# A hybrid attention layer: the compression's input tile stored with the blocks as its innermost axis

## The chip, the cores and the metric

The kernel runs on one core of a Trainium2 chip. The metric is device time in microseconds (us), the median of several executions. One more execution, taken with the hardware profiler, gives the rows below.

## The reference

One decoder layer over 512 tokens of width 1024. One projection of x feeds two token mixers: sparse attention (NSA), and gated DeltaNet. Their outputs are gated, summed and projected, then comes a gated MLP. The change is in the first branch of the sparse attention, the compression: of the 512 tokens, 31 blocks of 32 tokens are taken at a step of 16, so that neighbours overlap by half. Each block of 32 x 64 numbers, plus a learned position term, goes through a small two-layer network, once for keys (i = 0) and once for values (i = 1), in each of two groups of heads:

```
n_cmp = (S - CMP_LEN) // CMP_STRIDE + 1            # 31 blocks of 32 tokens, step 16
cmp_idx = np.arange(n_cmp)[:, None] * CMP_STRIDE + np.arange(CMP_LEN)[None, :]
def compress(t, i):
    blk = t[:, :, cmp_idx] + cmp_pos[i]
    blk = blk.reshape(B, G, n_cmp, CMP_LEN * DH)
    return jax.nn.gelu(blk @ cmp_w1[i]) @ cmp_w2[i]
k_cmp, v_cmp = compress(kc, 0), compress(vc, 1)
```

## The kernel before

The engines are named as in the profile: PE is TensorE (PEld its weight load), DVE is VectorE, ACT is ScalarE, POOL is GpSimd, SP is SyncE, which issues the DMAs.

The input projection is made in units of 128 output columns (gemm_t): a weight tile (raw) comes by DMA, is split into a high and a low part (wh on ACT or DVE at L215/L217, wl on DVE or POOL at L219), and 24 matmuls of 512 columns (lines 229, 231 and 232) build one product in a PSUM tile gps. The steps of the two mixers are listed in the table ORDER with priorities, and a scheduler lays them out in one fixed sequence on each engine. Units of the projection whose results are wanted later fill PE between the steps of the mixers. An engine works through its sequence in order, and waits where an operand or a buffer isn't ready.

The step "c" is the compression (compressed, in the code below). Two units of the projection (16 for the keys, 17 for the values) leave 128 rows by 512 tokens each in PSUM. Eight copies on ACT (lines 666 and 667, four for each unit) bring them into the tile kv: a head group's 64 rows as they are into partitions 0 to 63, and the same rows moved by one token into partitions 64 to 127. So one column of kv holds two neighbouring tokens, and a block of 32 tokens is 16 such columns. The fifth slice of kv holds the position terms and zeros. Line 674 then makes 16 matmuls, one for each j, that add up in one PSUM tile (ph in the code, aps in the profile): the weights are w1[j], and the moving operand is 5 slices of kv with 31 columns each, 155 in all, taken 16 elements (64 bytes) apart. Operands are float32, and each matmul stands in the trace as two records of MATMUL and two of LDWEIGHTS, so 32 of each. The two w1 tiles sit in the pool's raw buffers.

What hangs on ph is a chain: the position terms (hb, L678), bias (cu, L681), GELU (L684 to L688), the copies gv (L691), the second layer (L695 and L701, on PE), and its copies kcb and vcb.

Around it in the sequence stands the first head of the DeltaNet mixer: gdn_mid multiplies keys by keys and by queries (L466, two halves of two matmuls with 256 columns each), whose results DVE takes as m and at (L468, L469). They share a pool of two PSUM buffers (dps) with the transposes of the decay (L386), which ACT reads at L459 (dt). gdn_tri then inverts a triangular matrix: lo and f (L478, L480), gx (L486), a matmul of gx (L488), its copy lx (L489), and 15 dependent steps on DVE (L495 and L496), which end in z (L498) and its transposes on PE (L386).

Of the kernel before, what the change touches and what calls it, by code (L numbers as in the profile page):

```python
# [10 lines left out]
F32 = mybir.dt.float32  # L11
F32R = mybir.dt.float32r
AF = mybir.ActivationFunctionType
# [4 lines left out]
S = 512  # L18
# [112 lines left out]
def body(ctx: ExitStack, tc: tile.TileContext, d, out):  # L131
    nc = tc.nc
    V, A, G, PE = nc.vector, nc.scalar, nc.gpsimd, nc.tensor

    def E(name, h, d="V"):

        return {"V": V, "G": G, "A": A}[ENGINE.get(f"{name}{h}", d)]

    def bc(ap, shape):
        return ap.to_broadcast(shape)  # L140
# [64 lines left out]
    def split_w(src, shape, eng, first=A):  # L205

        raw = wp.tile(shape, F32, name="raw", bufs=BUFS["raw"])
        nc.sync.dma_start(out=raw, in_=src)
        half = shape[1] // 2
        hi, lo = [], []  # L210
        for i in range(2):
            r = raw[:, i * half:(i + 1) * half]
            wh = wp.tile([128, half] + list(shape[2:]), F32R, name="wh", bufs=BUFS["wh"])
            if first is A:
                A.activation(wh, r, AF.Copy)  # L215
            else:
                first.tensor_copy(wh, r)  # L217
            wl = wp.tile([128, half] + list(shape[2:]), F32R, name="wl", bufs=BUFS["wl"])
            eng.tensor_tensor(wl, r, wh.bitcast(F32), op=OP.subtract)  # L219
            hi += [wh[:, k] for k in range(half)]  # L220
            lo += [wl[:, k] for k in range(half)]
        return hi, lo

    def product(ps, w, m, n):

        (wh, wl), (mh_, ml_) = w, m
        first = None
        for k in range(n):
            i = PE.matmul(ps, wh[k], mh_(k), start=(k == 0), stop=False)  # L229
            first = first or i  # L230
            PE.matmul(ps, wh[k], ml_(k), start=False, stop=False)  # L231
            PE.matmul(ps, wl[k], mh_(k), start=False, stop=(k == n - 1))  # L232
        return first
# [3 lines left out]
    def gemm_t(u, eng=None, after=None):  # L237
        w = split_w(d["wT"][u], [128, KD, 128], E("ws", u, "G"), E("wh", u, "A"))
        ps = gps()
        first = product(ps, w, (lambda k: xh[:, k, :], lambda k: xl[:, k, :]), KD)  # L240
        if after is not None:
            tc.add_manual_dep(first.ins, after.ins.name, mybir.DependencyInfo(
                mybir.DependencyClass.NoSync, mybir.DependencyReason.SCHED_ONLY), reason="its rows have no room before")
        return ps
# [407 lines left out]
    def compressed():  # L652
        cst_ = ExitStack()
        ct = pool(cst_, name="ct", bufs=1, side="left")
        kv = ct.tile([128, 5, S], F32, name="kv")
        w2 = nsa.tile([128, 128], F32, name="w2")
        nc.sync.dma_start(out=w2, in_=d["w2"])
        pos = nsa.tile([128, 2, 16], F32, name="pos")
        nc.sync.dma_start(out=pos, in_=d["pos"])
        V.memset(kv[:, 4, :], 0.0)  # L660
        V.tensor_copy(kv[:, 4, :64].rearrange("p (i j two) -> p i j two", i=2, two=2)[:, :, :, 0], pos)
        for i in range(2):
            ps = gemm_t(16 + i)
            for g in range(2):
                own = slice(g * 64, g * 64 + 64)
                A.activation(kv[0:64, 2 * i + g, :], ps[own], AF.Copy)
                A.activation(kv[64:128, 2 * i + g, 0:S - 1], ps[own, 1:S], AF.Copy)
        w1 = []
        for i in range(2):
            w1.append(wp.tile([128, 8, 128], F32, name="raw", bufs=BUFS["raw"]))  # L670
            nc.sync.dma_start(out=w1[i], in_=d["w1"][:, 8 * i:8 * i + 8].rearrange("p a b c -> p a (b c)"))
        ph = aps()
        for j in range(16):
            PE.matmul(ph[:, :155].rearrange("p (a n) -> p a n", a=5), w1[j // 8][:, j % 8],
                      kv[:, :, 2 * j:2 * j + 481:16], start=(j == 0), stop=(j == 15))
        cst_.close()
        hb = nsa.tile([128, 2], F32, name="hb")
        V.tensor_copy(hb[0:64, 0:1], ph[0:64, 124:125])  # L678
        V.tensor_copy(hb[64:128, 0:1], ph[64:128, 126:127])
        u = nsa.tile([128, 62], F32, name="cu")  # L680
        A.activation(u[0:64], ph[0:64, 0:62], AF.Identity, bias=hb[0:64, 0:1])  # L681
        A.activation(u[64:128], ph[64:128, 62:124], AF.Identity, bias=hb[64:128, 0:1])
        t = nsa.tile([128, 62], F32, name="ct")
        V.tensor_tensor(t, u, u, op=OP.mult)  # L684
        V.tensor_scalar(t, t, 0.044715, 1.0, op0=OP.mult, op1=OP.add)
        V.tensor_tensor(t, t, u, op=OP.mult)
        A.activation(t, t, AF.Tanh, scale=GELU_C)
        V.scalar_tensor_tensor(u, t, 1.0, u, op0=OP.add, op1=OP.mult)  # L688
        gv = nsa.tile([128, 2, 4, 32], F32, name="gv")
        V.memset(gv, 0.0)  # L690
        V.tensor_copy(gv[64:128, :, :, 0:31],  # L691
                      bc(u[64:128].rearrange("p (g n) -> p g n", g=2)[:, :, None, :], (64, 2, 4, 31)))
        V.memset(kcb, 0.0)
        pk = aps()
        PE.matmul(pk[:, :62], w2[0:64], u[0:64], start=True, stop=True)  # L695
        for g in range(2):
            A.activation(kcb[0:64, g, 0:31], pk[0:64, 31 * g:31 * g + 31], AF.Copy, scale=0.5)
            A.activation(kcb[64:128, g, 32:63], pk[64:128, 31 * g:31 * g + 31], AF.Copy, scale=0.5)
        pv = aps()
        for g in range(2):  # L700
            PE.matmul(pv[:, 64 * g:64 * g + 64], gv[64:128, g].rearrange("p a b -> p (a b)"), w2[64:128, 0:64],  # L701
                      start=True, stop=True)
        for g in range(2):
            A.activation(vcb[:, g, 0, :], pv[:, 64 * g:64 * g + 64], AF.Copy, scale=0.5)
            V.scalar_tensor_tensor(vcb[:, g, 1, :], pv[:, 64 * g:64 * g + 64], 0.5,
                                   vcb[:, g, 0, :].bitcast(F32), op0=OP.mult, op1=OP.subtract)
# [140 lines left out]
    for step in ORDER:  # L847
        f = {"c": compressed, "k": keys, "q": queries, "p": cmp_attn, "a": lambda h: attn(h, (0, 1, 2)), "b": lambda h: attn(h, (3, 4, 5)),
             "i": gdn_k, "j": gdn_q, "v": gdn_v, "m": gdn_mid, "n": gdn_tri, "y": gdn_gate,
             "o": gdn_out, "g": lambda i: merge(i, mgp)}[step[0]]  # L850
        with tc.high_priority(offset=-(at + SHIFT.get(step, 0))):
            p0 = tc.tile_snap_priority()
            f(*[int(i) for i in step[1:]])
            at += tc.tile_snap_priority() - p0
        if step == "c":
            yo = pool(early, name="yo", bufs=1, side="left")
            mgp = pool(early, name="mg", bufs=1, side="left")
# [28 lines left out]
    for m in range(8):  # L886
# [5 lines left out]
        for b in range(2):  # L892
            ps = pm.tile([128, S], F32, name=f"pm{b}")
# [61 lines left out]
    for t in range(TT):  # L955
# [6 lines left out]
        for i in range(2):  # L962
            if i == 1 and t:
                x1_both(t - 1)
            ps = pw.tile([128, S], F32, name=f"pw{i}")
# [39 lines left out]
    for p in range(NF):  # L1005
        g = []
        for b in range(2):
            if p < NE:
                ps = first[p, b][2]
            else:  # L1010
                wu = split_w(d["up"][p, :, b], [128, KD, 128], V)
                ps = pu.tile([128, S], F32, name=f"pu{b}")
# [4 lines left out]
            for i in (1, 0):  # L1017
                n = 2 - i
# [72 lines left out]
```

## Time and profile before

| | |
|---|---|
| median of 3 runs | 876.38 us (875.93, 876.38, 881.3) |
| the profiled execution | 879.48 us |
| its span, first to last instruction | 877.7 us |
| granted clock of TensorE, mean over the span | 0.988 of full speed |

The profiled execution spends 1.8 us outside its span. Its rows are times from the start of the span. A matmul's row gives its start and a length that reaches past the start of the next one, since matmuls are pipelined: what one of them costs PE is the distance from one start to the next, called pitch below.

### The profile page before, as it was taken

The page shows a single profiled execution, that of the slowest core. Times are in us where ns is not written, and L with a number is a line of the kernel's source. Part 1 is how long each engine was busy: PE and PEld are TensorE (multiplying, and loading weights), DVE is VectorE, ACT ScalarE, POOL GpSimd, SP SyncE. Part 2 cuts the span into 40 slices and gives each one's busy share as a digit, 9 for nine tenths or more (in the row PEclk, how much of TensorE's full clock was granted, in tenths as well). Part 3 has the DMA queues.
Part 4 walks back from the last instruction along what each step waited for, and adds up shares of the span by engine and source line. Part 5 has one row for each costly group of instructions (what it writes and reads, how often), then busy time and mean ns, then how long its engine had stood idle before and what let it go on. Part 6 is the DMA issues. An engine that isn't in the chain of part 4 may idle for free.

```text
span 877.7 us, 11725 instructions
## 1 busy us (share of the span) xinstructions
PE 847.1 (97%) x4292; PEld 698.2 (80%) x4292; DVE 562.6 (64%) x1159; ACT 384.8 (44%) x855; POOL 159.9 (18%) x141
## 2 busy tenths in 40 slices
PE   9899799999999999999999999999999999999996
PEld 8677678777777678888888898888888888888885
DVE  4755759995766987485457636777766677423337
ACT  5463268567446767443234104444444444322220
POOL 1232342324424320112100001111111111000001
PEclk9999799999999999999999999999999999999999
DMA  7323110101111001254356001333333323333322
GB/s 244 119 72 96 48 50 25 49 25 49 48 50 48 25 26 49 73 159 137 135 192 240 24 1 49 96 96 97 96 97 98 97 98 98 106 100 99 96 73 96
DMA packets 22954, 76.33 MB, mean 87 GB/s; under 512 B 3184, under 2 KB 3568, under 8 KB 22640
## 3 DMA queue, kind: packets, MB, share of 16 engines
q1 hardware_dynamic: 22896, 75.57, 26.9%
q8 instruction: 34, 0.56, 0.2%
q14 instruction: 24, 0.20, 0.1%
HBM read 73.47 MB, written 2.10 MB: 86 GB/s over the span
## 4 chain that ended last, share of the span: by engine, by line
PE 86%; DVE 9%; ACT 2%; issue 1%; DMA 1%; POOL 0%; SPq 0%; DVEq 0%; ACTq 0%; POOLq 0%
PE pu L229 9%; PE pu L231 9%; PE pu L232 9%; PE gps L229 7%; PE gps L232 7%; PE gps L231 7%; PE pdn L1036 5%; PE pdn L1034 5%; PE pdn L1035 5%; PE pout L805 2%; DVE tmp L495 2%; PE pw L969 2%; PE pw L970 2%; PE pm L232 2%; PE pm L231 2%; PE pw L968 2%
## 5 line engine op out<-in xcount | busy, mean ns | idle before, releaser
L215 ACT ACTIVATE wh<-raw 128x512 fp32r<-128x512 f32 (+1 forms) x198 | 122.6, 622 | 224.4 <-PE pu L231 99.3
L219 DVE TENSOR_TENSOR wl<-raw,wh 128x512 fp32r<-128x512 f32 (+1 forms) x172 | 134.5, 784 | 133.4 <-ACT wh L215 130.5
L229 PE MATMUL pu<-mh,wh 128*128 128x512 f32 (+1 forms) x384 | 142.7, 372 | 0.0
L231 PE MATMUL pu<-ml,wh 128*128 128x512 f32 (+1 forms) x384 | 142.6, 371 | 0.0
L232 PE MATMUL pu<-mh,wl 128*128 128x512 f32 (+1 forms) x384 | 142.6, 371 | 0.0
L229 PE MATMUL gps<-xh,wh 128*128 128x512 f32 x320 | 131.3, 411 | 0.8 <-DVE acc L372 0.5
L232 PE MATMUL gps<-xh,wl 128*128 128x512 f32 x320 | 130.4, 407 | 0.0
L231 PE MATMUL gps<-xl,wh 128*128 128x512 f32 x320 | 129.0, 403 | 0.0
L219 POOL TENSOR_TENSOR wl<-raw,wh 128x512 fp32r<-128x512 f32 x48 | 63.5, 1324 | 170.5 <-ACT wh L215 101.0
L232 PEld LDWEIGHTS pu<-mh,wl 128*128 128x128 f32 x384 | 72.3, 188 | 12.6
L229 PEld LDWEIGHTS pu<-mh,wh 128*128 128x128 f32 x384 | 72.3, 188 | 12.6
L231 PEld LDWEIGHTS pu<-ml,wh 128*128 128x128 f32 x384 | 72.3, 188 | 12.3
L1019 DVE SCALAR_TENSOR_TENSOR fa<-pu,fcw,fa 128x511 f32<-128x511 f32 x88 | 65.7, 746 | 10.7 <-ACT fa L1016 9.2
L229 PEld LDWEIGHTS gps<-xh,wh 128*128 128x128 f32 x320 | 61.3, 191 | 12.9 <-issue 1.3
L232 PEld LDWEIGHTS gps<-xh,wl 128*128 128x128 f32 x320 | 61.0, 191 | 11.2 <-POOL wl L219 0.5
L231 PEld LDWEIGHTS gps<-xl,wh 128*128 128x128 f32 x320 | 61.1, 191 | 10.6 <-issue 0.4
L1025 POOL TENSOR_TENSOR fth<-fth,fa 128x512 f32<-128x512 f32 x22 | 28.7, 1302 | 214.0 <-DVE fa L1019 214.0
L1035 PE MATMUL pdn<-wl,ah 128*128 128x512 f32 x144 | 56.0, 389 | 0.0
L1034 PE MATMUL pdn<-wh,ah 128*128 128x512 f32 x144 | 56.0, 389 | 0.0
L1036 PE MATMUL pdn<-wh,al 128*128 128x512 f32 x144 | 56.0, 389 | 0.0
L765 ACT ACTIVATE sc<-sc,mn 128x384 f32<-128x384 f32 (+2 forms) x64 | 35.7, 559 | 15.0 <-DVE mn L763 14.3
L247 POOL TENSOR_TENSOR rs<-rs,minus_half 128x1 f32<-128x1 f32 x8 | 7.5, 941 | 184.3 <-DVE rs L929 184.3
(295 smaller groups left out, 1536.8 us busy)
## 6 DMA issues: line engine op xcount, KB each, us to landing
raw<-in_up SPq DMA_DIRECT2D x44, 512.0 KB, 3.6
raw<-in_wT SPq DMA_DIRECT2D x40, 512.0 KB, 3.6
raw<-in_down SPq DMA_DIRECT2D x22, 512.0 KB, 3.4
raw<-in_wm SPq DMA_DIRECT2D x8, 512.0 KB, 3.7
raw<-in_wo SPq DMA_DIRECT2D x8, 512.0 KB, 3.5
xr<-in_xT SPq DMA_DIRECT2D x8, 256.0 KB, 4.9
ln<-in_lnr SPq DMA_DIRECT2D x2, 1024.0 KB, 5.5
xax<-in_x SPq DMA_DIRECT2D x4, 512.0 KB, 5.2
```

Of the source, the lines that this page charges most:

```text
L215: A.activation(wh, r, AF.Copy)
L219: eng.tensor_tensor(wl, r, wh.bitcast(F32), op=OP.subtract)
L229: i = PE.matmul(ps, wh[k], mh_(k), start=(k == 0), stop=False)
L231: PE.matmul(ps, wh[k], ml_(k), start=False, stop=False)
L232: PE.matmul(ps, wl[k], mh_(k), start=False, stop=(k == n - 1))
L495: V.tensor_tensor(tmp[:, :, :n], lx[:, :, r + 1:, r], bc(xs[:, :, r:r + 1], (128, TT, n)), op=OP.mult)
L765: A.activation(s[:, i, :n], s[:, i, :n], AF.Exp, scale=-1.0, bias=mn[:, 0, i:i + 1], accum_out=mn[:, 1, i:i + 1])
L1019: V.scalar_tensor_tensor(acc[:, n:], ps[:, :S - n], w[:, i:i + 1], acc[:, n:], op0=OP.mult, op1=OP.add)
L1025: G.tensor_tensor(th, th, g[1], op=OP.mult)
L1034: PE.matmul(ps, ah[:, k, ts], wh, start=(k == 0), stop=False)
L1035: PE.matmul(ps, ah[:, k, ts], wl, start=False, stop=False)
L1036: PE.matmul(ps, al[:, k, ts], wh, start=False, stop=(k == NF - 1))
```

## The change

The tile kv gets another layout: instead of 512 tokens in a row it holds, for each of 8 values of j, the 32 groups of 16 tokens one beside the other. The moving operand of each matmul is then 5 runs of 31 neighbouring elements. The copies on ACT do the reordering: each of the eight now reads 256 elements of PSUM 16 elements apart (two axes, 8 by 32) and writes 256 in a row, where it read 512 (or 511) in a row before. For j from 8 to 15 the matmul reads the slice of j - 8, from its second element on. The fill of the position terms (L660, L661) gets the same layout.

```diff
@@ -652,19 +652,21 @@
     def compressed():
         cst_ = ExitStack()
         ct = pool(cst_, name="ct", bufs=1, side="left")
-        kv = ct.tile([128, 5, S], F32, name="kv")
+
+        kv = ct.tile([128, 5, 8, 32], F32, name="kv")
         w2 = nsa.tile([128, 128], F32, name="w2")
         nc.sync.dma_start(out=w2, in_=d["w2"])
         pos = nsa.tile([128, 2, 16], F32, name="pos")
         nc.sync.dma_start(out=pos, in_=d["pos"])
-        V.memset(kv[:, 4, :], 0.0)
-        V.tensor_copy(kv[:, 4, :64].rearrange("p (i j two) -> p i j two", i=2, two=2)[:, :, :, 0], pos)
+        V.memset(kv[:, 4], 0.0)
+        V.tensor_copy(kv[:, 4, :, 0:4], pos.rearrange("p i (h j) -> p j (i h)", j=8))
         for i in range(2):
             ps = gemm_t(16 + i)
+            pairs = ps.rearrange("p (n j two) -> p two j n", two=2, j=8)
             for g in range(2):
                 own = slice(g * 64, g * 64 + 64)
-                A.activation(kv[0:64, 2 * i + g, :], ps[own], AF.Copy)
-                A.activation(kv[64:128, 2 * i + g, 0:S - 1], ps[own, 1:S], AF.Copy)
+                for two in range(2):
+                    A.activation(kv[64 * two:64 * two + 64, 2 * i + g], pairs[own, two], AF.Copy)
         w1 = []
         for i in range(2):
             w1.append(wp.tile([128, 8, 128], F32, name="raw", bufs=BUFS["raw"]))
@@ -672,7 +674,7 @@
         ph = aps()
         for j in range(16):
             PE.matmul(ph[:, :155].rearrange("p (a n) -> p a n", a=5), w1[j // 8][:, j % 8],
-                      kv[:, :, 2 * j:2 * j + 481:16], start=(j == 0), stop=(j == 15))
+                      kv[:, :, j % 8, j // 8:j // 8 + 31], start=(j == 0), stop=(j == 15))
         cst_.close()
         hb = nsa.tile([128, 2], F32, name="hb")
         V.tensor_copy(hb[0:64, 0:1], ph[0:64, 124:125])
```

The sequences of the engines change at this place only. On PE, aps<-kv,raw are the 16 matmuls in question, dps<-kq the second half of gdn_mid's products, and gps<-xh,.. those of the projection. Before:

```order
L231 MATMUL gps<-xl,wh 128x512
L466 MATMUL dps<-kq 128x256 x2
L232 MATMUL gps<-xh,wl 128x512
L674 MATMUL aps<-kv,raw 128x155 x8
L229 MATMUL gps<-xh,wh 128x512
L674 MATMUL aps<-kv,raw 128x155
L231 MATMUL gps<-xl,wh 128x512
L674 MATMUL aps<-kv,raw 128x155
```

With the change:

```order
L231 MATMUL gps<-xl,wh 128x512
L466 MATMUL dps<-kq 128x256
L676 MATMUL aps<-kv,raw 128x155 x2
L466 MATMUL dps<-kq 128x256
L676 MATMUL aps<-kv,raw 128x155 x5
L232 MATMUL gps<-xh,wl 128x512
L676 MATMUL aps<-kv,raw 128x155
L229 MATMUL gps<-xh,wh 128x512
L676 MATMUL aps<-kv,raw 128x155
```

Seven of the 16 matmuls now stand ahead of one product of the projection, two of them between the last two dps<-kq, and eight behind it alternate with the projection. On ACT, kv<-gps are the last four copies (those of unit 17), dm and dt belong to gdn_mid, and wh is the split of a weight tile. Before:

```order
L453 ACTIVATE dm<-dps 128x512
L666 ACTIVATE kv<-gps 64x512
L667 ACTIVATE kv<-gps 64x511
L459 ACTIVATE dt<-dps 128x512
L666 ACTIVATE kv<-gps 64x512
L667 ACTIVATE kv<-gps 64x511
L215 ACTIVATE wh<-raw 128x512 x2
```

With the change:

```order
L453 ACTIVATE dm<-dps 128x512
L669 ACTIVATE kv<-gps 64x256 x3
L459 ACTIVATE dt<-dps 128x512
L669 ACTIVATE kv<-gps 64x256
L215 ACTIVATE wh<-raw 128x512 x2
```

Three of these copies, not two, now stand ahead of dt. On DVE one split (wl, L219) moves ahead of the second pair of m and at (L468, L469). Behind these places the sequences hold the same operations in the same order up to the end, and those of POOL and of the DMA queue are the same throughout.

## Rows read from the trace of the kernel before

**Rows 1.** The page, part 4: the chain that ended last, by engine.

```profile
PE 86%; DVE 9%; ACT 2%; issue 1%; DMA 1%; POOL 0%; SPq 0%; DVEq 0%; ACTq 0%; POOLq 0%
```

**Rows 2.** Windows: busy us (x instructions) by engine, granted clock, DMA share, GB/s.

```profile
73.20:79.60 6.40, 6.40 (x27) 5.08 (x26) 0.00 (x0) 0.41 (x1) 0.43 (x1) 1.00 0.30 84
```

**Rows 3.** Timeline of PE, 65 to 80 us: start, length, tile, shape, count [idle before].

```profile
66.19 1.03 PE L466 MATMUL dps<-kq 128*128 128x256 f32 x4
...
67.92 1.13 PE L466 MATMUL dps<-kq 128*128 128x256 f32 x4 [0.24 <-ACT dt L459]
...
69.14 4.46 PE L674 MATMUL aps<-kv,raw 128*128 128x155 f32 x16
...
73.68 0.69 PE L674 MATMUL aps<-kv,raw 128*128 128x155 f32 x2
```

**Rows 4.** Timeline of PE, later: what follows that group, and contiguous 64 columns.

```profile
79.75 0.39 PE L229 MATMUL gps<-xh,wh 128*128 128x512 f32 x1
...
82.58 0.32 PE L695 MATMUL aps<-cu,w 64*128 64x62 f32 x1
...
83.17 1.56 PE L488 MATMUL dps<-gx,cst 128*128 128x512 f32 x4
...
118.25 1.22 PE L715 MATMUL aps<-kcb,qf 128*128 128x64 f32 x10
```

**Rows 5.** Groups by shape, PE: busy us, mean ns of one (its own length).

```profile
L674 PE MATMUL aps<-kv,raw 128*128 128x155 f32 x32 | 10.0, 438 | 0.0
...
L466 PE MATMUL dps<-kq 128*128 128x256 f32 x32 | 8.5, 388 | 0.2 <-ACT dt L459 0.2
...
L715 PE MATMUL aps<-kcb,qf 128*128 128x64 f32 x32 | 4.0, 268 | 0.0
```

**Rows 6.** The chain that ended last, 50 to 120 us: start, length, what.

```profile
73.84 0.53 PE aps L674 x2
...
99.44 1.65 DVE z L498
101.23 1.09 PE dps L386 x4
```

**Rows 7.** Waits, 55 to 92 us: who waited for what, us in total, times, longest.

```profile
POOL wl L219 <- PE aps L695: 9.4, 1, 9.4
DVE hb L678 <- PE aps L674: 6.6, 1, 6.6
```

**Rows 8.** Timeline of ACT around the second set of copies.

```profile
66.06 0.59 ACT L666 ACTIVATE kv<-gps 64x512 f32<-64x512 f32 x1 [0.66 <-PE gps L232]
...
67.27 0.60 ACT L459 ACTIVATE dt<-dps 128x512 f32<-128x512 f32 x1
...
68.50 0.59 ACT L667 ACTIVATE kv<-gps 64x511 f32<-64x511 f32 x1
```

**Rows 9.** Groups by shape, ACT: busy us, mean ns of one.

```profile
L538 ACT ACTIVATE x<-dps 64x256 f32<-64x256 f32 x4 | 1.5, 373 | 2.0 <-PE dps L536 1.8
```

**Rows 10.** Groups by shape, DVE, 70 to 130 us: reductions over 512 elements.

```profile
L480 DVE TENSOR_REDUCE f<-lo 128x64 f32<-128x512 f32 x1 | 1.0, 1008 | 0.0
...
L721 DVE TENSOR_REDUCE cmx<-cs 128x16 f32<-128x512 f32 x1 | 0.7, 676 | 0.0
```

**Rows 11.** Timeline of DVE and POOL around the tile gx.

```profile
69.09 0.42 DVE L468 TENSOR_TENSOR m<-dps,db 128x256 f32<-128x256 f32 x1 [0.77 <-PE dps L466]
...
69.78 1.69 DVE L219 TENSOR_TENSOR wl<-raw,wh 128x512 fp32r<-128x512 f32 x1
...
72.56 1.07 POOL L486 TENSOR_TENSOR gx<-f,cst 128x256 f32<-128x256 f32 x1
```

**Rows 12.** Windows around two idle times of PE; PEclk is the granted clock.

```profile
95.70:101.20 5.50, 0.00 (x0) 0.00 (x1) 5.14 (x11) 1.72 (x3) 2.59 (x3) 0.86 0.32 95
101.30:109.80 8.50, 8.50 (x47) 7.42 (x47) 3.16 (x6) 0.91 (x3) 1.30 (x2) 0.50 0.00 1
...
243.00:246.40 3.40, 3.40 (x15) 3.00 (x15) 2.15 (x5) 0.60 (x1) 0.00 (x0) 0.50 0.51 155
```

## The prediction

> **What bounds the kernel now.** I read the shares of the chain that ended last first: 86% of it lies on PE [rows 1], so a microsecond of PE's own work counts unless PE would have waited anyway. Then I looked for the 16 matmuls of line 674 in the windows, the timeline, the waits and the chain. From 69 to 80 us PE works on them and on one product of the projection between them, without an idle moment. In the window 73.2 to 79.6 us PE is busy all the time at the full clock (2.4 GHz), while DVE does nothing and ACT 0.4 us [rows 2]. The reader should see that the others wait for exactly this: DVE 6.6 us for the end of the sum ph, POOL 9.4 us for the second layer behind it [rows 7]. The pieces of line 674 stand in the chain too [rows 6].
>
> What one of these records costs is the distance from start to start. The first 16 begin at 69.14 and fill 4.46 us, the last with its own length of 0.44 us, so the pitch is (4.46 - 0.44) / 15 = 0.268 us [rows 3, 5]. The other 16 stand in pairs that take 0.52 to 0.53 us in the chain, 0.264 us each, eight such pairs [rows 6]. Together: 16 x 0.268 + 16 x 0.264 = 8.5 us.
>
> For contiguous float32 columns, the same trace has two neighbours. Four records of line 466 with 256 columns: (1.03 - 0.38) / 3 = 0.217 us, the last one's length being 0.38 [rows 3, 5]; the mean of all in rows 5 is 0.39. Ten of line 715 with 64 columns: (1.22 - 0.27) / 9 = 0.106 us [rows 4, 5]. Half of 0.217 is 0.108, so 64 columns cost what 128 would, and under some 0.106 us a record with weights of its own doesn't come here. For 256 contiguous columns the cost is 0.85 ns a column, or 2 cycles at 2.4 GHz. Line 674 pays 0.268 / 155 = 1.7 ns a column, or 4 cycles: twice as much. Nothing else in the row explains this, neither the clock [rows 2] nor a wait [rows 3]; what sets these matmuls apart is the step of 16 elements in the moving operand and that it comes in five runs.
>
> **The change, part by part.** *The matmuls.* If the step is the reason, a record of 155 columns costs 155 / 256 x 0.217 = 0.131 us. 32 records: 4.2 us, against 8.5: a gain of **4.3 us** on PE. The ends of this term: 32 x 0.106 = 3.4 us if only the floor counts (gain 5.1), and no gain at all if the five runs and not the step are what costs. I take 0.131, since the row of 256 columns is the same type of operand at the same clock, a few microseconds earlier.
>
> *The copies.* Eight stay eight, but each moves 256 elements for 512. ACT took 0.59 us for 512 [rows 8], and takes 0.37 us for 64x256 read contiguously from PSUM [rows 9]. The new ones read PSUM 16 elements apart, and no row shows ACT do that. The nearest row of a strided read is DVE's reduction L480, which reads SBUF 16 elements apart: 1.01 us for 512 elements, where a contiguous reduction takes 0.68 [rows 10], so 0.33 us more for 512 and 0.17 for 256. Ends: 0.37 and 0.37 + 0.17 = 0.54 us; below 0.37 I see no reason. I take the lower end, because it is ACT itself, the same memory and the same size. Of the first four (unit 16) nobody waits for the end. The last four stand around dt, for which PE waits [rows 3]: they begin at 66.06 when the projection's product ends, and dt starts at 67.27 after two of them [rows 8]. With the change three go ahead: 66.06 + 3 x 0.39 (0.37 and a gap of 0.02, as between the old ones) = 67.23, the same. With 0.54 a copy, dt starts at 67.74, 0.47 us late, and PE's work behind it moves by that. The fourth copy ends near 68.2 in the one case and 68.9 in the other, as the first of PE's two matmuls dps<-kq behind dt ends (67.9 or 68.4, and two records at (1.13 - 0.38) / 3 = 0.25 us). So PE's first 674 waits for nothing or for a few hundredths. Cost of the copies: 0 to 0.5 us, taken as 0.
>
> *The changed order.* Seven matmuls move ahead of a projection matmul, two of them between the last dps<-kq; PE does the same sum. What comes later by it is the second pair of m and at, by 4 records (0.5 us), and, since one split moves ahead on DVE, by about 1.5 us in all: before it starts at 69.09 [rows 11]; now the split, which waits for ACT's wh after the copies (some 68.9 us), goes first and takes up to 1.7 us. Behind m hang f and gx, whose last part POOL ends at 73.6 [rows 11]; it would end near 75.1. The matmul that needs gx starts at 83.17 [rows 4], and with the change near 78.9: a cover of 9.5 us that shrinks to 3.8. Free. The fill of the position terms is half as large and lies long before: free.
>
> *Who is late next.* Behind the group PE has twelve projection matmuls, from 79.75 on, before the second layer at 82.58 [rows 4]. They cover the chain hb, cu, GELU, gv on DVE and ACT, which starts when ph ends; both start 4.3 us earlier, so the cover stays. The DMAs that refill the w1 buffers are released by these matmuls and move with them. Then gx's matmul, lx and DVE's 15 steps end in z at 101.1, for which PE waits 5.5 us [rows 6, 12]; that chain is started by PE's own order at 83.17, so it moves by the same 4.3 us, and with it everything later.
>
> **The sum.** 879.48 (the profiled execution: span 877.7 and 1.8 around it) - 4.3 + 0 = 875.2 us for a like execution. That execution was 3.1 us above the median of the runs shown, so against the median: 876.4 - 4.3 = **872.1 us**, 0.5% less. A measurement of this kernel tells about 1% (8.8 us) from no change, by which this counts as no change.
>
> **The rivals.** *The strided columns were not the price.* If the five runs or the odd length of 31 cost the second half of the pitch, PE keeps 8.5 us and the time stays at 876.2 (ACT's copies alone win nothing that PE waits for). For it: no row here has runs and columns enough to part the two. Against: 4 cycles a column is a clean double, while five run starts would have to cost 0.027 us each.
>
> *The gain is lost on the way.* A chain that doesn't move with PE, such as DVE's 15 steps, or a weight tile that comes late: 873 to 876.4, with 875.5 as its middle. Against it stand the waits, which name PE [rows 7].
>
> *The clock.* PE idles from 95.7 to 101.2 us, and right behind, from 101.3 to 109.8, its granted clock is 0.50 (1.2 GHz, the lower level); a later stretch of 3.4 us at 243 shows 0.50 too [rows 12]. The idle time moves by 4 us, and the low stretch may come out shorter or longer. All 8.5 us at the full clock would give back at most 4.3; one more stretch such as that at 243 would cost 1.7. The runs of before lie 5.4 us apart, which fits this size. Time: 868 to 874, or up to 877 if the executions that count are the slow ones.
>
> *Slower: ACT's strided reads of PSUM.* They stand before dt and before the first 674, and PE has nothing to do meanwhile. If a copy takes X us, dt ends at 66.67 + 3X instead of 67.88, and the fourth copy a further X later, of which 0.5 us lies beside PE's two records: a loss of 3X - 1.2 + X - 0.5 = 4X - 1.7 us. From X = 1.5 us on (6 ns an element, four times the contiguous row) it eats the gain. At X = 2 it is 6.3 us, and the first four copies add up to 4 more in front of the splits of weights: 876.4 - 4.3 + 8 = 880 us. In favour: it is the one access that the trace doesn't show. Against: DVE's strided read costs half more, not four times. The Trainium skill (PSUM — Partial Sum Buffer, Specifications) speaks against the change here: it gives PSUM lines of 8 bytes and says that any non-contiguous pattern slows matmuls significantly. It names no price and no ScalarE read, and no run here shows either; if the rule held for ACT this rival would be the result.
>
> **How the numbers follow.** Forecast (gain carried, 872.1, with ACT's copies up to 872.6): 0.64. Strided columns not the price, 876.2: 0.10. Gain lost on the way, about 875.5: 0.12. Clock, a shift of more than 2 us either way: 0.09, half below 870 and half above 874. ACT's reads, 880: 0.05. The range reaches from 872.1 - 0.8 (the floor's 5.1 for 4.3) - 2.2 (half of what the clock can give back) - 0.5 (the two lower runs of before lie that far apart) = 868.6 to 877.0, which takes in the cases at 875.5 and 876.2; outside are the ACT case and the ends of the clock's. Faster than 867.6 needs the whole clock gain on top: 0.04. Slower than 885.1 needs ACT copies near 3 us: 0.02. Within 1%: 0.94.
>
> **What would show it.** In the changed kernel's trace: the pitch of line 676 at 0.13 us, with the length from the first start to the last about 4.3 us shorter; copies of 64x256 at 0.37 to 0.54 us; the wait of DVE's hb for PE down from 6.6 to some 2; gx ready by 75.5 and its matmul near 79; z's end near 97 and PE's idle time before it again 5.5 us. A pitch that stays at 0.26 brings down the first step, a copy above 1 us the second, and an idle time before z's transposes that has grown by what was won the last.

## The result, and the profile after

The changed kernel takes 873.4 us, the median of 14 runs; the kernel before took 880.36 us, the median of 14 runs beside them. The ratio is 0.9938 with a 95% interval of 0.992 to 0.9956: between 3.9 and 7.0 us less. One of the changed kernel's 14 runs took 2091.85 us, for a reason that no trace shows; it counts in the median, which is 873.17 us without it, and not in the ratio. The profiled execution took 875.11 us with a span of 873.3 us, 4.4 us less than the span before. Both profiled executions have the same mean granted clock, 0.988.

The timeline of PE, where [rows 3, 4] stood. Line 676 is the old 674, and 697 the old 695:

```profile
67.63 0.70 PE L466 MATMUL dps<-kq 128*128 128x256 f32 x2 [0.21 <-ACT dt L459]
68.17 0.69 PE L676 MATMUL aps<-kv,raw 128*128 128x155 f32 x4
...
69.13 1.48 PE L676 MATMUL aps<-kv,raw 128*128 128x155 f32 x10
...
70.67 0.43 PE L676 MATMUL aps<-kv,raw 128*128 128x155 f32 x2
...
77.97 0.32 PE L697 MATMUL aps<-cu,w 64*128 64x62 f32 x1
...
78.56 1.56 PE L488 MATMUL dps<-gx,cst 128*128 128x512 f32 x4
```

The group of these matmuls by shape (busy us, mean ns of one, idle before):

```profile
L676 PE MATMUL aps<-kv,raw 128*128 128x155 f32 x32 | 6.0, 294 | 0.0
```

Ten records of line 676 take 1.48 us, of which the last one's own 0.29, so the pitch is (1.48 - 0.29) / 9 = 0.132 us, where it was 0.268. The second layer starts at 77.97 and not at 82.58, and gx's matmul at 78.56 and not at 83.17: both 4.6 us earlier. The waits that hung on this group, as in [rows 7]:

```profile
POOL wl L219 <- PE aps L697: 5.0, 1, 5.0
...
DVE hb L680 <- PE aps L676: 2.1, 1, 2.1
```

DVE's wait for the sum has shrunk by 4.5 us and POOL's by 4.4. The copies on ACT, as in [rows 8]: three of them in one row, then dt, the fourth, and the next split.

```profile
65.80 1.16 ACT L669 ACTIVATE kv<-gps 64x256 f32<-64x256 f32 x3 [0.66 <-PE gps L232]
66.98 0.60 ACT L459 ACTIVATE dt<-dps 128x512 f32<-128x512 f32 x1
67.60 0.38 ACT L669 ACTIVATE kv<-gps 64x256 f32<-64x256 f32 x1
68.01 0.63 ACT L215 ACTIVATE wh<-raw 128x512 fp32r<-128x512 f32 x1
```

Their group by shape (busy us, mean ns of one, idle before), to be held against [rows 9]:

```profile
L669 ACT ACTIVATE kv<-gps 64x256 f32<-64x256 f32 x8 | 3.0, 376 | 0.8 <-PE gps L232 0.7
```

A copy that reads PSUM 16 elements apart takes 0.376 us; the contiguous one of the same size took 0.373. The chain that ended last, as in [rows 6]:

```profile
70.83 0.26 PE aps L676 x2
...
94.83 1.65 DVE z L498
96.62 1.09 PE dps L386 x4
```

A pair of line 676 takes 0.26 us in the chain where it took 0.53, z ends at 96.5 us where it ended at 101.1, and its transposes start at 96.62 where they started at 101.23. The windows around the two idle times, as in [rows 12]:

```profile
91.10:96.50 5.40, 0.00 (x0) 0.00 (x0) 5.13 (x11) 1.72 (x3) 2.54 (x2) 0.89 0.32 97
96.70:105.40 8.70, 8.70 (x47) 7.62 (x48) 3.20 (x6) 1.12 (x4) 1.29 (x2) 0.50 0.00 1
...
238.70:242.00 3.30, 3.30 (x15) 2.91 (x14) 2.07 (x4) 0.60 (x1) 0.00 (x0) 0.50 0.47 148
```

The whole picture is moved: PE idle from 91.1 to 96.5, then the granted clock at 0.50 for as long as before, and again at 238.7. From there to the end the distance stays at 4.3 to 4.4 us. The first matmul of the MLP, before and with the change:

```profile
508.88 0.28 PE L229 MATMUL pu<-mh,wh 128*128 128x256 f32 x1
```

```profile
504.50 0.28 PE L229 MATMUL pu<-mh,wh 128*128 128x256 f32 x1
```

The span ends 4.4 us earlier.

### The profile page after: what moved, and what is told of

It reads as the page before. It is cut to its first block, busy times and chain, and to the rows that moved or that the text cites. A ratio compares the mean times of both kernels' runs of the same rounds, so it can differ in the third digit from the quotient of the medians.

```text
span 873.3 us, 11725 instructions
## 1 busy us (share of the span) xinstructions
PE 843.2 (97%) x4292; PEld 696.7 (80%) x4292; DVE 564.1 (65%) x1159; ACT 383.2 (44%) x855; POOL 159.1 (18%) x141
## 4 chain that ended last, share of the span: by engine, by line
PE 86%; DVE 9%; ACT 3%; issue 1%; DMA 0%; POOL 0%; DVEq 0%; SPq 0%; ACTq 0%; POOLq 0%
PE pu L229 9%; PE pu L232 9%; PE pu L231 9%; PE gps L229 7%; PE gps L232 7%; PE gps L231 7%; PE pdn L1038 5%; PE pdn L1036 5%; PE pdn L1037 5%; PE pout L807 2%; DVE tmp L495 2%; PE pw L971 2%; PE pw L972 2%; PE pm L232 2%; PE pw L970 2%; PE pm L229 2%
## 5 line engine op out<-in xcount | busy, mean ns | idle before, releaser
L219 DVE TENSOR_TENSOR wl<-raw,wh 128x512 fp32r<-128x512 f32 (+1 forms) x172 | 134.9, 786 | 134.3 <-ACT wh L215 131.4
L219 POOL TENSOR_TENSOR wl<-raw,wh 128x512 fp32r<-128x512 f32 x48 | 63.5, 1325 | 166.4 <-ACT wh L215 97.5
```

## The experiments

Six kernels ran. Four of them keep the sequences of the changed kernel on every engine, so that their rows can be compared place by place. As a common measure I take the distance from the start of L450, a matmul of gdn_mid ahead of the copies (dps<-grh), to the start of the second layer, because L450 itself starts up to 1.2 us apart in these executions. The starts are read from the timeline of each. L450 before, and with the change:

```profile
63.92 0.39 PE L450 MATMUL dps<-grh,upper_r 128*128 128x512 f32 x1
```

```profile
63.67 0.39 PE L450 MATMUL dps<-grh,upper_r 128*128 128x512 f32 x1
```

**The copies and the new order, without the matmuls' part (copies_alone).** The old layout, but only the tokens that the matmuls read are copied:

```diff
-                A.activation(kv[0:64, 2 * i + g, :], ps[own], AF.Copy)
-                A.activation(kv[64:128, 2 * i + g, 0:S - 1], ps[own, 1:S], AF.Copy)
+                for two in range(2):
+                    A.activation(kv[64 * two:64 * two + 64, 2 * i + g, 0:S:2], ps[own, two:S:2], AF.Copy)
```

> The old layout of the tile with its step of 16 elements in the matmuls, but each copy moves only the 256 tokens that the matmuls read (every second one), so copies are as short as in the changed kernel and the sequences of all engines are those of the changed kernel. If the step alone carries the gain (my theory): pitch of line 674 stays at 0.264 to 0.268 us, span within 0.5 us of the kernel before, ratio 0.999 to 1.001. If shorter copies or the other order carry a part of it: the span falls by 1 us or more (ratio 0.998 or less) at an unchanged pitch.

Ratio 1.0021 against the kernel before (0.9992 to 1.005, so no gain), span 877.2 us. Its timeline of PE:

```profile
69.06 2.80 PE L674 MATMUL aps<-kv,raw 128*128 128x155 f32 x10
...
81.61 0.32 PE L695 MATMUL aps<-cu,w 64*128 64x62 f32 x1
```

The pitch is (2.80 - 0.435) / 9 = 0.263 us (0.435 us is the group's mean), and the second layer follows L450 (63.02) after 18.59 us, where it was 18.66 before and is 14.30 with the change. Shorter copies and the new order are worth 0.07 us. The gain is the matmuls'.

**How far apart may the columns be (step2, step3, step4).** The changed kernel with n elements between neighbours, for n = 2, 3 and 4; for n = 2:

```diff
-        kv = ct.tile([128, 5, 8, 32], F32, name="kv")
+        kv = ct.tile([128, 5, 8, 32, 2], F32, name="kv")
...
-                    A.activation(kv[64 * two:64 * two + 64, 2 * i + g], pairs[own, two], AF.Copy)
+                    A.activation(kv[64 * two:64 * two + 64, 2 * i + g, :, :, 0], pairs[own, two], AF.Copy)
...
-                      kv[:, :, j % 8, j // 8:j // 8 + 31], start=(j == 0), stop=(j == 15))
+                      kv[:, :, j % 8, j // 8:j // 8 + 31, 0], start=(j == 0), stop=(j == 15))
```

(The position terms are stored in the same places.)

> The changed kernel with the 31 elements of each run 2 elements (8 bytes) apart, copies as long as before it, same sequences. Theory A, any step but 1 halves the rate: pitch 0.264, the gain of 4.3 us is gone (ratio near 1.000). Theory B, what counts is how many elements of a 16-byte line are used (the Trainium skill, SBUF - State Buffer, Door 1, says two hits in a line keep full rate): pitch 0.132, ratio near 0.995, as the changed kernel. Theory C, the five runs or the length of 31 set the old pitch: it is refuted already if the changed kernel's pitch of 0.132 stays here.

> As step2 with 3 elements (12 bytes) between neighbours: a run meets a new 16-byte line at three of four elements. Theory A (any step): pitch 0.264. Theory B (lines of 16 bytes, an element that is alone in its line pays): in every 48 bytes two elements are alone and two share a line, so between: about 0.2 us. If it is 0.132, the price begins only at a step of 4.

> As step2 with 4 elements (16 bytes) between neighbours, one element in each 16-byte line. Theories A and B both: pitch 0.264, all of the 4.3 us lost, ratio near 1.000 although copies and order are those of the changed kernel. If the price depended on the distance itself (64 bytes being worse than 16): pitch between 0.132 and 0.264 and a ratio between 0.995 and 1.

Step2 gave a ratio of 0.9967 (0.9947 to 0.9987), step4 1.0024 (1.0005 to 1.0042), step3 ran once (877.26 us, span 875.4). From each, a row of PE's timeline, and the groups of the matmuls and of the copies. Step2:

```profile
69.46 1.56 PE L676 MATMUL aps<-kv,raw 128*128 128x155 f32 x10
```

```profile
L676 PE MATMUL aps<-kv,raw 128*128 128x155 f32 x32 | 6.3, 303 | 0.0
```

```profile
L669 ACT ACTIVATE kv<-gps 64x256 f32<-64x256 f32 x8 | 3.1, 393 | 0.8 <-PE gps L232 0.7
```

Step3:

```profile
68.94 2.20 PE L676 MATMUL aps<-kv,raw 128*128 128x155 f32 x10
```

```profile
L676 PE MATMUL aps<-kv,raw 128*128 128x155 f32 x32 | 8.6, 379 | 0.0
```

```profile
L669 ACT ACTIVATE kv<-gps 64x256 f32<-64x256 f32 x8 | 4.1, 507 | 0.8 <-PE gps L232 0.7
```

Step4:

```profile
70.00 2.93 PE L676 MATMUL aps<-kv,raw 128*128 128x155 f32 x10
```

```profile
L676 PE MATMUL aps<-kv,raw 128*128 128x155 f32 x32 | 10.7, 452 | 0.0
```

```profile
L669 ACT ACTIVATE kv<-gps 64x256 f32<-64x256 f32 x8 | 5.0, 621 | 0.8 <-PE gps L232 0.7
```

By the same working, and with the copies and the distance from L450 to the second layer:

| step of the columns | pitch, us | a copy on ACT, us | start of L450, of the second layer | distance, us |
|---|---|---|---|---|
| 1 (the change) | 0.132 | 0.376 | 63.67, 77.97 | 14.30 |
| 2 | 0.140 | 0.393 | 63.91, 78.58 | 14.67 |
| 3 | 0.202 | 0.507 | 62.70, 80.01 | 17.31 |
| 4 | 0.275 | 0.621 | 63.01, 82.91 | 19.90 |
| 16 (copies_alone) | 0.263 | 0.392 | 63.02, 81.61 | 18.59 |
| 16 (before) | 0.268, 0.264 | 0.59 | 63.92, 82.58 | 18.66 |

The runs settle two things. Theory C is out: five runs of 31 columns stand in every one of these kernels, and at step 1 they cost 155 x 2 cycles at 2.4 GHz (0.129 us) and 3 ns. Theory A is out: step 2 costs 8 ns, not 0.13. Theory B gave the form: two elements in each 16 bytes are nearly free, one alone in its 16 bytes costs as much as two, and step 3, where half of the elements are alone, lies halfway (0.202 between 0.132 and 0.275). That is the rule that the Trainium skill states for SBUF (SBUF — State Buffer, Door 1), two hits in a 16-byte line for full bandwidth, and these traces agree with it for TensorE's moving operand, with the sizes that it doesn't give. The same passage of the Trainium skill gives 4 float32 elements as how far one can step for free; read as a step of 4, the traces don't agree: 3 costs 0.070 us a record, and 4 costs 0.143. A step of 64 bytes is no worse than one of 16. Steps between 4 and 16 weren't run. Why step 4 costs 0.012 us more than step 16 stays open.

Step4 also shows the rival that ended slower, at a small price. Its copies write kv 16 bytes apart and take 0.62 us. ACT's timeline:

```profile
65.15 1.89 ACT L669 ACTIVATE kv<-gps 64x256 f32<-64x256 f32 x3 [0.66 <-PE gps L232]
67.07 0.60 ACT L459 ACTIVATE dt<-dps 128x512 f32<-128x512 f32 x1
```

and PE's row behind dt:

```profile
67.72 0.70 PE L466 MATMUL dps<-kq 128*128 128x256 f32 x2 [0.94 <-ACT dt L459]
```

Three copies take 1.89 us and not 1.16, and PE's wait for dt grows from 0.21 us to 0.94: by 0.73, which is 3 x (0.621 - 0.376). The first matmul of line 676 starts 0.65 us behind the first dps<-kq and not 0.54, since the fourth copy ends later. So both parts of the prediction's formula for this stall hold at X = 0.62; the reads from PSUM just don't make X large.

**What the low clock costs (warm_before, warm_after).** In both kernels, matmuls whose result is overwritten fill PE's wait for z. The computation is complete in both.

```diff
+    def warm(ps, n, after):
...
+            m = PE.matmul(ps, ident, C["alibi"], start=True, stop=True)
...
         px = dps(c4)
+        if h == 0:
+            warm(px, 6, last)
         trans4(px, lambda c: z[:, c, :])
```

> The kernel before, with 6 float32 matmuls of 512 columns put in front of the transposes of the first head's z, whose result nobody reads (the transposes overwrite it); they fill about 5.1 of the 5.5 us in which PE waits for DVE. A part of the later sequence shifts by it. Clock theory (the low clock behind PE's idle time costs up to 4.3 us, and differs between executions): granted clock 1.00 from 96 to 110 us, span 2 to 4 us shorter, ratio 0.995 to 0.998, less spread between executions. Rival (the low clock is hidden, because DVE and ACT set the pace of the inversion there): clock 1.00 but span within 1 us. Rival (filler in the way): the matmuls end after z, and the span grows by up to 2 us.

> The changed kernel with the same filler and the same shift of the later sequence. My theory: it stands to warm_before as the sum of PE says, 4.3 us (0.5%) less, and the change's measured 5.5 us (ratio 0.9938) was 4.3 of matmuls and the rest how often the clock fell low for how long in the executions of either kernel. So ratio against the kernel before 0.990 to 0.993 if the clock theory holds. If instead the change itself brings 5.5 us: warm_after is 5.5 us below warm_before.

Warm_before came to 1.0071 (1.0046 to 1.0097), warm_after to 1.0021 (1.0003 to 1.0039): both slower than the kernel before, so neither is the better version that I had hoped for. PE's timeline of warm_before shows the first reason:

```profile
93.48 4.45 PE L249 MATMUL dps<-cst,ident 128*128 128x512 f32 x10
99.88 0.41 PE L520 MATMUL dps<-z,m 128*128 128x64 f32 x2 [1.95 <-DVE z L509]
100.13 1.83 PE L249 MATMUL dps<-cst,ident 128*128 128x512 f32 x2
101.76 1.06 PE L395 MATMUL dps<-ident,z 128*128 128x128 f32 x4
```

DVE's timeline of the same kernel, for the end of z:

```profile
98.10 1.64 DVE L509 TENSOR_TENSOR z<-xs,cst 128x512 f32<-128x512 f32 x1
```

Ten of the filler's 12 records end before z does (99.74 us), but the last two stand behind a matmul that needs z, and z's transposes start 2.0 us after z's end instead of 0.1: the rival "filler in the way". The windows behind it show the granted clock at 0.50 for 3.4 us instead of 8.5, and then at 1.00:

```profile
100.30:103.70 3.40, 3.40 (x12) 2.26 (x12) 0.00 (x0) 0.60 (x1) 0.00 (x0) 0.50 0.00 0
103.80:110.00 6.20, 6.20 (x59) 4.34 (x58) 3.66 (x8) 2.21 (x6) 1.29 (x1) 1.00 0.01 4
```

The next transposes of z, further down the inversion, show what that is worth. Before the change, where the first ones started at 101.23 [rows 6]:

```profile
108.09 1.06 PE L386 MATMUL dps<-ident,z 128*128 128x128 f32 x4
```

In warm_before, where the first ones started at 101.76:

```profile
106.20 0.60 PE L395 MATMUL dps<-ident,z 128*128 128x128 f32 x4
```

That is 6.86 us, all at the low clock, against 4.44 us, of which 2.0 at the low one: 2.4 us less. Two records of the matmul that stands ahead of the filler's end belong to this stretch in the kernel before; at 0.2 us each (eight take 1.60 us in the chain there) they are 0.4 of it. Some 2.0 us are the clock's, and the misplaced filler takes back 1.9. That is one trace: behind the same filler, warm_after's low stretch lasts 6.6 us, and the distance between its transposes is 6.07 us where the changed kernel has 6.86.

```profile
98.10:104.70 6.60, 6.60 (x28) 5.58 (x26) 2.26 (x4) 1.80 (x3) 1.27 (x1) 0.50 0.01 2
```

The second reason is the later sequence, which the filler shifted: the MLP's first matmul starts at 514.2 us in warm_before (508.9 before), although this stretch ended earlier. What that sequence costs in all is not worked out, but two spells at the low clock belong to it. One, from 178.8 us, is new: it comes behind a wait of PE of 2.4 us, and the kernel before ran at 1.00 there. The other lasts 6.6 us where [rows 12] show 3.4:

```profile
178.80:182.20 3.40, 3.40 (x10) 2.64 (x9) 3.19 (x22) 2.09 (x8) 0.00 (x0) 0.50 0.00 0
243.80:250.40 6.60, 6.57 (x27) 5.62 (x28) 3.25 (x8) 2.38 (x4) 0.00 (x0) 0.50 0.25 79
```

So the whole times say nothing clean about the clock, and only the stretch does.

A price without a filler stands in two traces above, of the change and of step4, whose engines work in the same order. Behind the same idle time of 2.75 us, the changed kernel's clock is at 0.50 for 3.3 us (the window from 238.7 to 242.0 above):

```profile
238.47 0.49 PE L386 MATMUL aps<-ident,cs 128*128 128x128 f32 x2 [2.75 <-DVE xs L496]
...
243.68 1.00 PE L512 MATMUL dps<-ym,x 128*128 128x64 f32 x8
```

Step4's stays at 1.00:

```profile
242.40 0.41 PE L386 MATMUL aps<-ident,cs 128*128 128x128 f32 x2 [2.75 <-DVE xs L496]
...
246.34 1.00 PE L512 MATMUL dps<-ym,x 128*128 128x64 f32 x8
```

```profile
242.00:246.00 4.00, 3.48 (x25) 3.07 (x26) 2.96 (x8) 1.20 (x2) 0.00 (x0) 1.00 0.43 131
```

The same matmuls take 5.21 us in the one and 3.94 in the other. Such a stretch costs 1.3 us, where the prediction's estimate was 1.7, and whether it comes is not fixed by the order of the instructions.

The warm pair among themselves has the same filler and the same later sequence, and it shows the change's gain again. From the matmul that was L450 to the second layer it is 18.66 us in warm_before (62.58 to 81.24) and 14.31 in warm_after (63.51 to 77.82): 4.35 us less. By the medians warm_after is 4.75 us below warm_before (880.28 and 885.03), and by the ratios 0.5% (1.0021 / 1.0071 = 0.995); the six runs of the one and the twelve of the other are spread over 3.3 and 5.8 us, too far to tell 4.3 from 5.5. The ratio of 0.990 to 0.993 that was expected of warm_after did not come.

## Why the prediction was right

**The matmuls.** 32 records at 0.132 us and not 0.131, in place of 8.5 us: the term of 4.3 us was right in mechanism and in size. The trace shows 4.35 us from L450 to the second layer (18.658 against 14.305 before rounding), and 4.4 at the end of the span. The reason given, 4 cycles a column against 2 for contiguous ones, was the step's: with the new layout, order and copies kept, a step of 4 brings the old pitch back.

**The copies.** Taken as free at 0.37 us each, measured 0.376. PE's wait for dt was 0.24 us before and is 0.21 now. The first 676 starts 0.54 us behind the first dps<-kq (67.63 to 68.17), as foreseen. The nearest row of a strided read, DVE's reduction from SBUF, was a misleading neighbour and rightly served only as the upper end. The line of the Trainium skill that the prediction held against the change (PSUM — Partial Sum Buffer, Specifications: a non-contiguous pattern slows matmuls) does not carry over to ScalarE's reads here: 0.376 us at a step of 64 bytes, 0.373 contiguously.

**The order.** The second m was said to be 1.5 us late and gx to be ready near 75.1. DVE and POOL around gx, as in [rows 11]:

```profile
68.67 0.69 DVE L219 TENSOR_TENSOR wl<-raw,wh 128x512 fp32r<-128x512 f32 x1 [0.63 <-ACT wh L215]
69.33 0.42 DVE L468 TENSOR_TENSOR m<-dps,db 128x256 f32<-128x256 f32 x1
```

```profile
72.38 1.06 POOL L486 TENSOR_TENSOR gx<-f,cst 128x256 f32<-128x256 f32 x1
```

This step of the prediction came out otherwise. The split took 0.69 us and not 1.7, since POOL isn't at work beside it now: in the trace before, the 132 splits of this size that DVE made with POOL idle took 0.63 to 0.69 us, and each one above 0.9 us had POOL at work beside it. So m is only 0.2 us late by the clock of the span (0.5 counted from L450), and gx ends at 73.4, where it ended at 73.6. The cover of 3.8 us was not needed; it is 5.1.

**Who is late next.** Nobody: DVE's wait for the sum is 2.1 us (2 foreseen), PE's idle time before z's transposes is 5.5 us as before, and the later places read above keep the distance. "The gain is lost on the way" had nothing to show for it.

**The sum.** 872.1 us was forecast and 873.4 measured. That they lie only 1.3 us apart is luck in part: the base was 4.0 us too low, and the medians differ by 2.7 us more than the 4.3 that was forecast. The three runs shown had a median of 876.38, the 14 of the comparison, with these three among them, 880.36, and those beside the experiments 878.05 (25 runs) and 878.65 (17). The profiled executions differ by 4.4 us, the two warm kernels by 4.75, the medians of the comparison by 7.0, where the interval of the ratio reaches from 3.9 to 7.0. What is beyond 4.4 isn't the change's work in any trace. It fits the clock: the changed kernel's executions, sorted by their mean granted clock, have spans of 869.7 to 870.7 us at 0.992, 870.6 to 871.9 at 0.990, 871.8 to 873.9 at 0.988 and 874.8 to 874.9 at 0.987 and 0.986. The clocks of 42 executions of the kernel before, those beside the experiments, allow a comparison at like clock: their median span lies above the changed kernel's by 4.0 us at 0.992 (873.9 and 869.9), by 5.0 at 0.990 (876.2 and 871.2) and by 4.1 at 0.988 (877.4 and 873.3). That the 14 executions of before had more of the long low stretches than these 42 is likely but not shown, since their clocks aren't listed.

## What to carry to other kernels

Look at the pitch of matmuls, start to start, against the columns: for float32 at the full clock the contiguous rows here paid 2 cycles a column and record, and 4 came from a moving operand that left all but one element of each 16 bytes unused. Let the copy that moves the data from PSUM to SBUF anyway do the reordering: reading PSUM with a large step cost ACT nothing here, while writing SBUF with a step of 16 bytes cost it 0.25 us in 256 elements. The gain on PE was kept in full here because the others waited for PE, and the waits told that beforehand.

## What was not expected of the hardware

ACT's copies were slowed by the step at which they write SBUF, not by the one at which they read PSUM: 0.376, 0.393, 0.507 and 0.621 us at a write step of 1, 2, 3 and 4 elements with the same read; at a write step of 2, a read step of 2 (copies_alone, 0.392) cost the same as one of 16. That is the same shape as TensorE's reads: nearly free at two elements in 16 bytes, and 0.96 ns more for each element when every one is alone. And the span of one and the same program varies by 5 us along with its mean granted clock, from 869.7 us at 0.992 to 874.9 us at 0.986, so that a change of 4.4 us needs the trace, or many runs, to be seen at its size.
